# A backbone of mLSTM, RWKV-7, RG-LRU and attention: the recurrence's steps and preparations numbered 300 ahead for every engine but TensorE

## The chip, the cores and the metric

The kernel runs on one core of a Trainium2 chip. The metric is the device time of one execution in microseconds; the kernel before is given by the median of three runs. A profiled execution of the same program gives the trace that is read here.

## The reference, cut to what matters

The kernel computes a two-layer backbone over 512 latent tokens and 256 context tokens of width 1024. Layer 0 projects its input once and feeds two mixers, an mLSTM and an RWKV-7 recurrence; their outputs are concatenated and projected; an MLP of width 4096 follows. Layer 1 has an RG-LRU and a neighbourhood attention in the same arrangement. The part that the change touches is the RWKV recurrence, with 8 heads of 64 in two directions (z), first over the context and then, from the context's state, over the latent tokens:

```python
def rwkv_run(r, v, decay, kk, k_dir, b_vec, S0):
    ...
    def step(S, inp):
        r_t, w_t, k_t, v_t, a_t, b_t = inp
        sa = jnp.einsum('zbhij,zbhj->zbhi', S, a_t)
        S = S * w_t[..., None, :] + sa[..., :, None] * b_t[..., None, :] + v_t[..., :, None] * k_t[..., None, :]
        return S, jnp.einsum('zbhij,zbhj->zbhi', S, r_t)
    S, y = lax.scan(step, S0, xs)
```

Context tokens share every weight with the latent ones: in layer 0 they have their own output projection and their own MLP pass.

## The kernel before, in words

All matrix products of the projections and MLPs are split into a high and a low part (`gemm`, L244): one weight tile of 128 x 1024 is loaded (L235), rounded on ScalarE to `wh` (L237), the rest is formed as `wl` on VectorE or GpSimd (L241), and TensorE then makes three products for each of 8 blocks of 128, that is 24 matmuls into one PSUM bank, of which there are two (`psg`). For the 256 context columns that bank is emptied by VectorE (L338 in output projections and the second half of the MLP, L383 in the first half).

The recurrence is cut into chunks of 64 tokens: 12 chunks, `s` = 0 to 3 for the context and 4 to 11 for the latent tokens, each for both directions. What a chunk needs from its own data alone is made in `pre(s)` (L839): loads from DRAM that `rwkv_in` wrote (L849 to L855), products `psA` (16 matmuls) that ScalarE copies (L861) and VectorE masks (L862, L863), then the inverse of 16 x 16 blocks. For it `AB` goes through DRAM (L868, L869) into `M` (L876), 15 pairs of small dependent operations follow (L890, L892; on GpSimd for `s` up to 4, on VectorE for the 7 chunks after), and the result `Xi` goes through DRAM again (L895) to `Xr` (L897), is transposed (L900) and widened to 64 x 64 by four groups of small matmuls `psI` with VectorE or ScalarE work between them (`dd` L910, `t` L918 and L920, `d1`, and `T` L939). `step(s)` (L949) then carries the state: `psC` products of `AS` and `X`, of `T` and `r`, of `BK` and `X` (the new state `S`, L968, L969), and of `Q` and `ar` for the output `ya_c` or `ya_l` (L985, L988). The tiles of a chunk lie in one of two sets, `s % 2`; those of the inverse exist once (pool `pr`).

Around this lies other work, the fillers (`fillers`, a generator): `rwkv_in(1)` (inputs of the latent chunks), the latent and the context output projection of the mLSTM half (`lat_mlstm`, `ctx_mlstm`), and `ctx_half`, which needs the recurrence's context output: its norms (`rwkv_norms`, L996 to L1004), the gate (`rwkv_gate`, L1024), the other half of the context's output projection, and the context's MLP. The loop over `s` pulls a set amount of filler (`PL`, 21 units from `s` = 3 on, where a context gemm of the MLP counts 2.6), then emits `step(s)`, `rwkv_norms(s)` and `pre(s + 1)`.

This emission order is not the order on the engines. When the program is closed, a scheduler walks a simulated timeline and gives each engine, among its instructions whose inputs are there, the one with the lowest number. The numbers count up in the order of emission. What comes out is one fixed queue for each engine and for the DMA issues of SyncE (SP), and the chip works each queue off in order.

The two lines of the loop that the change wraps are these:

```python
        S = step(s, X, S, Xn)
        rwkv_norms(s)
        ...
            pre(s + 1, Xn)
        X = Xn
        if s >= 3:
            pull(fill, PL[4])
```

Of the kernel before, what the change touches and what calls it, by code (L numbers as in the profile page):

```python
# [3 lines left out]

# [1 line left out]

# [12 lines left out]
P = 128  # L19
# [98 lines left out]
def hybrid_kernel(ctx: ExitStack, tc: tile.TileContext, A, out):  # L118
    WS = [int(x) for x in "2422"]
    nc = tc.nc  # L120
    uid = [0]

    def nm(s):
        uid[0] += 1
        return f"{s}_{uid[0]}"

    def after(ins, first):
        tc.add_manual_dep(ins.ins, first.ins.name,
                          mybir.DependencyInfo(mybir.DependencyClass.NoSync, mybir.DependencyReason.DATA),
                          reason="first matmul of the bank")  # L130

    def mm(o, l, r, start=True, stop=True, shared=False, tile=None):
        kw = {"tile_position": (32 * tile[0], 32 * tile[1])} if tile else {}
        return nc.tensor.matmul(o, l, r, start=start, stop=stop, skip_group_check=shared, **kw)  # L134

    pd = ctx.enter_context(tc.tile_pool(name="pd", bufs=1, space=bass.MemoryType.DRAM))
    pd2 = ctx.enter_context(tc.tile_pool(name="pd2", bufs=2, space=bass.MemoryType.DRAM))
# [9 lines left out]
    ident = C["ident"]  # L147
# [10 lines left out]
    def ada(layer, parts, pa, psa, tag):  # L158
        for pair, half in parts:
            ps = psa.tile([P, 256], F32, tag=tag, name=nm("psada"))  # L160
            for k0 in range(0, NK, 4):

                w = pa.tile([P, 4, D], F32, tag="adaw", name=nm("adaw"))
                for i in range(0, 4, 2):
                    nc.sync.dma_start(w[:, i:i + 2, :], A["ada_w"][layer, pair, half, (k0 + i) // 2])
                for i in range(4):
                    k = k0 + i
                    for j in range(4):
                        mm(ps[32 * j:32 * j + 32, :], sc[:, k, :], w[:, i, 256 * j:256 * j + 256], k == 0, k == NK - 1)
                yield 1.8  # L170
            rows = pa.tile([P, 256], F32, tag="rows", name=nm("rows"), bufs=1)
            nc.vector.tensor_copy(rows, ps)
            pt = psa.tile([P, 2, P], F32, tag=tag, name=nm("pst"))
            for t in range(2):
                nc.tensor.transpose(pt[:, t, :], rows[:, P * t:P * t + P], ident)
            src = pt.rearrange("p t (i j r) -> p i t j r", i=2, j=2)
            for i, idx in enumerate(PAIRS[pair]):
                o = 8 * idx + 4 * half
                dst = mod[:, layer, o:o + 4, :].rearrange("p (j t) c -> p t j c", t=2)
                bo = COLS["ada_b"][0] + 48 * layer + o  # L180
                bias = cols[:, bo:bo + 4].rearrange("p (j t) -> p t j", t=2)
                one = 1.0 if idx in (1, 4) else 0.0
                for cnd in range(2):
                    nc.vector.scalar_tensor_tensor(dst[:, :, :, cnd], src[:, i, :, :, cnd], one, bias, op0=ALU.add, op1=ALU.add)
# [228 lines left out]
    for i in (1, 0):  # L413
        n = SEGS[i][1]
# [87 lines left out]
    with tc.tile_pool(name="pg1", bufs=1) as pg1:  # L502
# [20 lines left out]
        for z in range(2):  # L523
# [37 lines left out]
            for c0, n in ((0, 4), (4, 2)):  # L561
                pt = psm.tile([P, n, P], F32, tag="m", name=nm("pst"))
# [126 lines left out]
    def rwkv_in(si, psp, psh, tag, last=None):  # L689
        off, n, _ = SEGS[si]  # L690
# [3 lines left out]
        fl = lambda a: a.rearrange("p c t -> p (c t)")  # L694
        with tc.tile_pool(name=nm("pha"), bufs=1) as pha, tc.tile_pool(name=nm("ph"), bufs=1) as ph, \
# [32 lines left out]
            for p in range(4):  # L728
                gup = ph.tile([P, P], F32, tag="gup", name=nm("gup"))
                nc.sync.dma_start(gup, A["g_up"][:, P * p:P * p + P])  # L730
                kk, k, r = (ph2.tile([P, nch, 64], F32, tag=a, name=nm(a)) for a in ("kk", "k", "r"))
                v = ph.tile([P, nch, 64], F32, tag="v", name=nm("v"))
# [31 lines left out]
                for z in range(2):  # L764
# [6 lines left out]
                    for kind in range(2):  # L771
# [4 lines left out]
                        o = 8 * z + 4 * kind + p  # L776
                        nc.scalar.activation(t_, pw, AF.Tanh, scale=0.5, bias=DV["upb"][:, o:o + 1])
                        th.append(t_)
                for z in range(2):
# [12 lines left out]
                    bk = ph.tile([P, nch, P], F32, tag="bk", name=nm("bk"))  # L792
# [11 lines left out]
                    nc.sync.dma_start(bkD[si][:, st, z, p, :], bk)  # L804
                pv = psh.tile([P, nb, P], F32, tag=tag, name=nm("psv"))
                for c in range(nb):
                    nc.tensor.transpose(pv[:, c, :], fl(v)[:, P * c:P * c + P], ident)
                vt = pha.tile([P, nb, P], F32, tag="zs", bufs=2, name=nm("vt"))
                nc.scalar.copy(vt, pv)
                nc.sync.dma_start(vD[si][:, p, :].rearrange("(c t) i -> t c i", t=P), vt)  # L810
# [24 lines left out]
    def bank(use, shape):  # L835
        pool, tag, bufs = banks[use]
        return pool.tile(shape, F32, tag=tag, bufs=bufs, name=nm("ps" + use))

    def pre(s, X):  # L839
# [5 lines left out]
        bk = pr2.tile([P, 2, 4, P], F32, tag="bk", name=nm("bk"))  # L845
# [7 lines left out]
        for z in range(2):  # L853
            c = 64 * (ch[z] - s0)
# [26 lines left out]
        for z in range(2):  # L881
            pt = bank("A", [P, 4, P])
            for p in range(4):
                nc.tensor.transpose(pt[:, p, :], bk[:, z, p, :], ident)
            nc.scalar.copy(BK[:, z], pt)
        eng = nc.gpsimd if s <= CT // CR else nc.vector
        for j in range(15):
            n, m = 15 - j, j + 1
# [37 lines left out]
        for p in range(4):  # L926
            for z, q in ((0, 0), (1, 0), (0, 1), (1, 1)):
                g, o = 2 * q + z, 2 * q + 1 - z
# [4 lines left out]
        for p in range(4):  # L933
            for z, q in ((0, 0), (1, 0), (0, 1), (1, 1)):
                o, g = 2 * q + z, 2 * q + 1 - z
# [10 lines left out]
    def new_x(s):  # L946
        return sets[s % 2].tile([P, 2, 4, 2, 64], F32, tag="X", name=nm("X"))

    def step(s, X, S0, Xn):  # L949
        ar, ge, Q, AS, BK, tt = PRE.pop(s)  # L950
        chunk = chunk_of(s)
        pR = bank("C", [P, 2, 4, 64])
        for z, p, q in UNITS:
            mm(pR[hs_[q], z, p, :], AS[:, z, p, q, :], X[:, z, p, q, :])
        r_ = pr.tile([P, 2, 4, 64], F32, tag="r", name=nm("r"))
        nc.scalar.copy(r_, pR)
        pU = bank("C", [P, 2, 4, 64])
        for z, p, q in UNITS:
            mm(pU[hs_[q], z, p, :], tt[z][hs_[q], p, :], r_[hs_[q], z, p, :])
        nc.scalar.copy(X[0:64, :, :, 0, :], pU[0:64])  # L960
        nc.vector.tensor_copy(X[0:64, :, :, 1, :], pU[64:P])
        S1 = None
        if s < NCR - 1:
            pS = bank("C", [P, 2, 4, 64])
            for z, p, q in UNITS:
                mm(pS[hs_[q], z, p, :], BK[:, z, p, hs_[q]], X[:, z, p, q, :])
            S1 = sets[(s + 1) % 2].tile([P, 2, 4, 64], F32, tag="S", name=nm("S"))
            nc.vector.tensor_tensor(S1, pS, S0, op=ALU.add)  # L968
            nc.vector.tensor_tensor(S1, S1, ge[:, :, :, None].to_broadcast([P, 2, 4, 64]), op=ALU.mult)  # L969
            nc.scalar.copy(Xn[0:64, :, :, 0, :], S1[0:64])  # L970
            nc.vector.tensor_copy(Xn[0:64, :, :, 1, :], S1[64:P])
        pY = bank("C", [P, 2, 4, 64])
        first = [None, None]
        for z, p, q in UNITS:
            i1 = mm(pY[hs_[q], z, p, :], Q[:, z, p, q, :], X[:, z, p, q, :], first[q] is None, False, shared=True)
            if first[q] is None:
                first[q] = i1
            else:
                after(i1, first[q])
        for z, p, q in UNITS:  # L980
            mm(pY[hs_[q], z, p, :], ar[hs_[q], z, p, 64:P], S0[hs_[q], z, p, :], False, False, shared=True)
        for z in range(2):
            d = ya_of(chunk[z])
            if chunk[z] in seen:
                nc.vector.tensor_tensor(d, pY[:, z], d, op=ALU.add)  # L985
            else:
                seen.add(chunk[z])
                nc.scalar.copy(d, pY[:, z])  # L988
        return S1
# [16 lines left out]
    def rwkv_norms(s):  # L1006

        si, last = (0, 3) if s < 4 else (1, 11)
        if s in (2, 3, 9, 11):
            v = YA[si].rearrange("p (g c) a i -> p g (c a) i", g=4)  # L1010
            for g in (slice(0, 4, 3) if s == last else slice(1, 3),) if si == 0 else (0, 3) if s == last else (1, 2):
                rwkv_norm(v[:, g] if si == 0 else v[:, g:g + 1])
# [64 lines left out]
    def pull(gen, us):  # L1077

        pos[1] += us
        while pos[0] < pos[1]:  # L1080
            t = next(gen, None)
            if t is None:
                pos[0] = pos[1]
                return
            pos[0] += t

    work = {str(h): mlstm_head(h) for h in range(HM)}
    work["c"] = rwkv_in(0, psg2, psm, "m")
    for o in "0000a0c1ccc1cc11c1c22cc2c23c12ccc33cR33":
        if o == "a":  # L1090
            bg[:] = [itertools.chain(ada(0, ((1, 0), (1, 1), (2, 0), (2, 1)), pa1, psa1, "ada"),
                                     ada(1, ((0, 0), (0, 1), (1, 0), (1, 1)), pa1, psa1, "ada")), 0.5, 0.0]
        elif o == "R":
# [7 lines left out]
            banks.update(A=(psh2, "h", 1), I=(psa1, "ada", 1))  # L1101
            S = sets[0].tile([P, 2, 4, 64], F32, tag="S", name="S0")
            nc.vector.memset(S, 0.0)
            X = new_x(0)
# [28 lines left out]
    for s in range(NCR):  # L1133
        if s < 4:
            pull(fill, PL[1 + s])
        while s == 3 and "in" not in done:
            pos[0] += next(fill)
        Xn = new_x(s + 1) if s + 1 < NCR else None
        while s == 4 and "lat" not in done:
            pos[0] += next(fill) or 0.0  # L1140
        S = step(s, X, S, Xn)
        rwkv_norms(s)
        if s == 3:
            done.add("ctx")
        if Xn is not None:
            pre(s + 1, Xn)
        X = Xn
        if s >= 3:
            pull(fill, PL[4])
# [353 lines left out]
```

## Time and profile before

| | |
|---|---|
| median of 3 runs | 2049.87 us (2041.36, 2049.87, 2053.16) |
| profiled execution | 2049.73 us, span of its trace 2047.9 us |
| TensorE matmul busy | 1925.2 us, 94% of the span |
| VectorE, ScalarE, GpSimd busy | 1052.2, 874.9, 870.1 us (51%, 43%, 42%) |
| mean granted TensorE clock | 0.965 of full |

The span runs from the first to the last instruction. Steps 0 to 11 of the recurrence lie between 432 and 945 us of it. Lines named L134 are the helper through which nearly all matmuls go, so the tiles tell which product it is. Matmuls are pipelined and their ends are modelled.

### The profile page before, as it was taken

The numbers are of one execution on the slowest core, as the hardware profiler recorded it, in microseconds if no ns is written. First come the engines' busy times: TensorE is split into PE (matmuls) and PEld (weight loads), VectorE is DVE, ScalarE is ACT, GpSimd is POOL, SyncE is SP. The second block draws the span as 40 slices with busy tenths as digits, with TensorE's granted clock in tenths as the row PEclk, the third lists the DMA queues.
The fourth block names the chain that finished last, engine by engine and source line by source line (L and its number), as shares of the span: only waits on it lengthen the run. The fifth ranks groups of instructions, "written<-read, shape, count | busy, mean of one in ns | idle before, by whom it ended". The sixth has DMA issues, their size and how long they took to land. (4 is left out here: it accounts for less than half of the span.)

```text
span 2047.9 us, 36663 instructions
## 1 busy us (share of the span) xinstructions
PE 1925.2 (94%) x14860; PEld 1593.9 (78%) x14860; DVE 1052.2 (51%) x1944; ACT 874.9 (43%) x1441; POOL 870.1 (42%) x708
## 2 busy tenths in 40 slices
PE   6899999899887999999999999999999899999998
PEld 5788786767577888888787888888766688888887
DVE  6773645676676766776541221243666664122122
ACT  4443445355544544444442332334655654233232
POOL 1455554435534222233244444435454454444444
PEclk9999998899888999999999999999989899999999
DMA  7356557454585555544443333325211222333232
GB/s 304 106 197 219 177 198 264 122 159 128 142 239 157 144 166 148 149 134 135 160 144 124 102 94 95 101 91 169 67 54 38 62 67 83 103 94 102 93 102 74
DMA packets 173864, 271.60 MB, mean 133 GB/s; under 512 B 77120, under 2 KB 115648, under 8 KB 168576
## 3 DMA queue, kind: packets, MB, share of 16 engines
q1 hardware_dynamic: 166608, 263.76, 41.4%
q10 hardware_dynamic: 7088, 5.51, 0.8%
q8 instruction: 117, 1.92, 0.4%
q14 instruction: 51, 0.42, 0.1%
HBM read 244.06 MB, written 25.17 MB: 131 GB/s over the span
## 5 line engine op out<-in xcount | busy, mean ns | idle before, releaser
L241 POOL TENSOR_TENSOR wl<-w,wh 128x1024 fp32r<-128x1024 f32 (+3 forms) x245 | 555.9, 2272 | 820.6 <-PE psg L134 435.7
L237 ACT CAST wh<-w 128x1024 fp32r<-128x1024 f32 (+3 forms) x319 | 313.2, 985 | 524.8 <-PE psg L134 460.1
L134 PE MATMUL psg<-xh,wh 128*128 128x512 f32 (+1 forms) x1440 | 500.3, 363 | 13.5 <-DVE k L710 3.0
L134 PE MATMUL psg<-xl,wh 128*128 128x512 f32 (+1 forms) x1440 | 498.5, 358 | 1.1 <-DVE xl L335 1.0
L134 PE MATMUL psg<-xh,wl 128*128 128x512 f32 (+1 forms) x1440 | 324.2, 356 | 0.0
L134 PEld LDWEIGHTS psg<-xh,wh 128*128 128x128 f32 x1440 | 273.5, 191 | 64.8 <-issue 13.3
L134 PEld LDWEIGHTS psg<-xl,wh 128*128 128x128 f32 x1440 | 275.7, 191 | 43.9 <-issue 4.9
L134 PEld LDWEIGHTS psg<-xh,wl 128*128 128x128 f32 x1440 | 243.5, 191 | 39.3 <-issue 3.5
L134 PE MATMUL psg<-hh,wh 128*128 128x512 f32 (+1 forms) x800 | 266.2, 350 | 6.4 <-DVE r L383 3.5
L134 PE MATMUL psg<-hl,wh 128*128 128x512 f32 (+1 forms) x800 | 268.1, 349 | 0.9 <-DVE hl L281 0.8
L338 DVE SCALAR_TENSOR_TENSOR res_l<-psg,mod,res_l 128x512 f32<-128x512 f32 (+1 forms) x108 | 74.3, 690 | 274.1 <-PE psg L134 274.0
L134 PEld LDWEIGHTS psg<-hh,wh 128*128 128x128 f32 x800 | 151.4, 190 | 27.8 <-issue 4.1
L134 PEld LDWEIGHTS psg<-hl,wh 128*128 128x128 f32 x800 | 151.7, 190 | 20.6 <-DVE hl L281 1.2
L134 PE MATMUL psg<-hh,wl 128*128 128x512 f32 (+1 forms) x800 | 166.0, 349 | 0.0
L134 PEld LDWEIGHTS psg<-hh,wl 128*128 128x128 f32 x800 | 132.4, 190 | 19.2
L383 DVE TENSOR_SCALAR r<-psg 128x512 f32<-128x512 f32 (+1 forms) x96 | 57.5, 600 | 171.4 <-PE psg L134 171.3
L281 DVE TENSOR_TENSOR hl<-r,hh 128x512 fp32r<-128x512 f32 (+1 forms) x96 | 86.8, 907 | 80.4 <-ACT hh L280 80.4
L384 ACT ACTIVATE r<-r 128x512 f32<-128x512 f32 (+1 forms) x96 | 53.6, 560 | 125.8 <-DVE r L383 125.8
L241 DVE TENSOR_TENSOR wl<-w,wh 128x1024 fp32r<-128x1024 f32 (+1 forms) x74 | 89.4, 1209 | 33.6 <-ACT wh L237 14.1
L134 PE MATMUL psada<-adaw,sc 128*32 128x256 f32 (+1 forms) x896 | 63.0, 386 | 8.4 <-DMA adaw<-in_ada_w_dram 4.8
L134 PE MATMUL psA<-ar,bk 64*128 64x128 f32 x384 | 51.0, 294 | 7.4 <-issue 4.2
L280 ACT CAST hh<-r 128x512 fp32r<-128x512 f32 (+1 forms) x96 | 52.6, 550 | 2.8
(423 smaller groups left out, 2857.6 us busy)
## 6 DMA issues: line engine op xcount, KB each, us to landing
w<-in_w_dram SPq DMA_DIRECT2D x192, 512.0 KB, 3.7
adaw<-in_ada_w_dram SPq DMA_DIRECT2D x40, 1024.0 KB, 7.4
w<-in_ev_in_dram SPq DMA_DIRECT2D x47, 512.0 KB, 3.7
w<-in_od_in_dram SPq DMA_DIRECT2D x32, 512.0 KB, 3.6
adaw<-in_ada_dram SPq DMA_DIRECT2D x16, 512.0 KB, 11.3
w<-in_out_w_dram SPq DMA_DIRECT2D x32, 256.0 KB, 2.9
bk<-bkD SPq DMA_DIRECT2D x12, 512.0 KB, 6.4
ar<-arD SPq DMA_DIRECT2D x12, 512.0 KB, 4.6
```

The costliest lines, as they stand in the source:

```text
L134: return nc.tensor.matmul(o, l, r, start=start, stop=stop, skip_group_check=shared, **kw)
L237: nc.scalar.copy(wh, w)
L241: eng.tensor_tensor(wl, w, wh.bitcast(F32), op=ALU.subtract)
L280: nc.scalar.copy(h, x)
L281: nc.vector.tensor_tensor(l, x, h.bitcast(F32), op=ALU.subtract)
L338: nc.vector.scalar_tensor_tensor(r_, ps, modcol(layer, idx, m, cnd), r_, op0=ALU.mult, op1=ALU.add)
L383: nc.vector.tensor_scalar(r_, ps, 0.0, None, op0=ALU.max)
L384: nc.scalar.activation(r_, r_, AF.Square)
```

## The change

`ahead(n)` opens a block in which the counter that numbers instructions is set back by `n`; at its end the counter is put back to where it stood before the block. `step` and `pre` are emitted in such blocks with `n` = 300. Inside them each matmul (and the two kinds of transposes on TensorE that `rwkv_in` and `pre` make) is emitted in a block of its own with the opposite offset, so that it gets the counter without the 300. No instruction is added, removed or changed in shape. Two things follow from the counter being put back. A matmul that goes through `mm`, anywhere in the kernel, no longer moves the counter on. And what is emitted after `step` or `pre` starts from the number at which that block began.

```diff
+    lead = [0]
+
+    @contextmanager
+    def ahead(n):
+
+        lead[0] = n
+        with tc.high_priority(offset=n):
+            yield
+        lead[0] = 0
+
     def mm(o, l, r, start=True, stop=True, shared=False, tile=None):
         kw = {"tile_position": (32 * tile[0], 32 * tile[1])} if tile else {}
-        return nc.tensor.matmul(o, l, r, start=start, stop=stop, skip_group_check=shared, **kw)
+        with tc.high_priority(offset=-lead[0]):
+            return nc.tensor.matmul(o, l, r, start=start, stop=stop, skip_group_check=shared, **kw)
...
                 for c in range(nb):
-                    nc.tensor.transpose(pv[:, c, :], fl(v)[:, P * c:P * c + P], ident)
+                    with tc.high_priority(offset=-lead[0]):
+                        nc.tensor.transpose(pv[:, c, :], fl(v)[:, P * c:P * c + P], ident)
...
             for p in range(4):
-                nc.tensor.transpose(pt[:, p, :], bk[:, z, p, :], ident)
+                with tc.high_priority(offset=-lead[0]):
+                    nc.tensor.transpose(pt[:, p, :], bk[:, z, p, :], ident)
...
-        S = step(s, X, S, Xn)
+        with ahead(300):
+            S = step(s, X, S, Xn)
         rwkv_norms(s)
         if s == 3:
             done.add("ctx")
         if Xn is not None:
-            pre(s + 1, Xn)
+            with ahead(300):
+                pre(s + 1, Xn)
```

## Rows read from the trace of the kernel before

**Rows 1.** The page's first part: busy time of each engine over the span.
```profile
span 2047.9 us, 36663 instructions
...
PE 1925.2 (94%) x14860; PEld 1593.9 (78%) x14860; DVE 1052.2 (51%) x1944; ACT 874.9 (43%) x1441; POOL 870.1 (42%) x708
```

**Rows 2.** Busy time by stretch: length, engines, granted clock, DMA share, GB/s.
```profile
400.00:675.00 275.00, 238.28 (x2822) 190.18 (x2823) 186.98 (x344) 130.06 (x234) 121.62 (x213) 0.91 0.56 160
675.00:945.00 270.00, 258.32 (x3930) 240.60 (x3929) 182.54 (x442) 120.31 (x205) 68.98 (x38) 0.99 0.53 148
```

**Rows 3.** TensorE's waits from 400 to 675 us: total us, times, longest.
```profile
PE psg L134 <- DVE gb L1024: 4.9, 1, 4.9
PE psg L134 <- ACT xhom L280: 4.6, 1, 4.6
PE psI L134 <- DMA Xr<-invD: 4.6, 3, 2.9
...
PE psA L134 <- DVE ms L997: 2.4, 1, 2.4
PE psI L134 <- DVE t L920: 2.3, 1, 2.3
```

**Rows 4.** TensorE's waits from 675 to 945 us.
```profile
PE psg L134 <- DVE r L383: 3.5, 3, 1.7
PE psI L134 <- DMA Xr<-invD: 2.9, 3, 1.7
PE psC L134 <- DVE X L961: 1.8, 1, 1.8
PE psC L134 <- DVE T L939: 1.4, 1, 1.4
```

**Rows 5.** Timeline of TensorE around chunk 3: start us, us, instruction.
```profile
560.83 0.65 PE L134 MATMUL psI<-Xt,AB 32*32 32x32 f32 x32
...
568.48 0.45 PE L134 MATMUL psI<-Xt,dd 32*32 32x32 f32 x32
568.75 0.48 PE L134 MATMUL psI<-Xr,dd 32*32 32x32 f32 x32
...
588.82 1.15 PE L134 MATMUL psC<-r,T 64*64 64x64 f32 x32
...
593.75 1.15 PE L134 MATMUL psC<-X,BK 128*64 128x64 f32 x32
```

**Rows 6.** Timeline of VectorE around chunk 3.
```profile
562.84 0.41 DVE L910 TENSOR_TENSOR dd<-psI,cst 128x256 f32<-128x256 f32 x1
...
573.83 0.28 DVE L918 TENSOR_TENSOR t<-psI,Xt 128x128 f32<-128x128 f32 x1
...
584.45 0.60 DVE L939 SCALAR_TENSOR_TENSOR T<-psI,cst,T 128x128 f32<-128x128 f32 x2
...
599.11 0.69 DVE L968 TENSOR_TENSOR S<-psC,S 128x512 f32<-128x512 f32 x1
```

**Rows 7.** Timeline of VectorE over one inverse of a latent chunk.
```profile
817.97 2.25 DVE L890 TENSOR_TENSOR tm<-M,Xi 64x15 f32<-64x15 f32 x1 [3.34 <-DMA M<-dA]
...
824.04 0.22 DVE L892 TENSOR_TENSOR Xi<-Xi,tm 64x63 f32<-64x63 f32 x1
824.30 0.22 DVE L890 TENSOR_TENSOR tm<-M,Xi 64x64 f32<-64x64 f32 x1
...
830.97 2.19 DVE L892 TENSOR_TENSOR Xi<-Xi,tm 64x28 f32<-64x28 f32 x1
...
833.40 0.17 DVE L892 TENSOR_TENSOR Xi<-Xi,tm 64x15 f32<-64x15 f32 x1
```

**Rows 8.** Timeline of GpSimd at the same place.
```profile
830.72 2.40 POOL L241 TENSOR_TENSOR wl<-w,wh 128x1024 fp32r<-128x1024 f32 x1 [10.54 <-ACT wh L237]
```

**Rows 9.** Timeline of TensorE inside a context gemm.
```profile
817.40 0.28 PE L134 MATMUL psg<-hh,wh 128*128 128x256 f32 x1
817.52 0.28 PE L134 MATMUL psg<-hl,wh 128*128 128x256 f32 x1
```

**Rows 10.** TensorE's groups by shape from 945 to 980 us: busy us, mean ns, idle before.
```profile
L134 PE MATMUL psg<-hl,wh 128*128 128x256 f32 x60 | 15.5, 293 | 0.1
```

More of the change, by code (lines that the diff above doesn't have):

```diff
@@ L2 @@
 import math
-from contextlib import ExitStack
+from contextlib import ExitStack, contextmanager
 import numpy as np
```

## The prediction

> **What bounds the kernel now.** I read the page's first part, then the busy times by stretch, then who TensorE waits for, then the timelines of TensorE and VectorE around one chunk of the recurrence. The first shows TensorE with a matmul under way for 94% of the span and every other engine at about half [rows 1]. So the end is set by TensorE's work and by the stretches in which it has none, and since the change adds and removes no instruction, only those stretches and TensorE's clock can move.
>
> By stretch, the 545 us in which the recurrence runs fall in two [rows 2]. From 400 to 675 us (chunks 0 to 3, with the latent inputs and the two first output projections as filler) TensorE is idle 275 - 238.3 = 36.7 us, and its mean granted clock is 0.91: (1 - 0.91) x 275 = 24.8 us of full-clock time are lost between the levels of 2.4 and 1.2 GHz. From 675 to 945 us (chunks 4 to 11, with the context's MLP as filler) it is idle 270 - 258.3 = 11.7 us at a clock of 0.99. In this second stretch TensorE itself is nearly full: a chunk takes 270 / 8 = 34 us, and the recurrence being quicker would only exchange filler for filler.
>
> The Trainium skill ("Trainium Kernel Development and Optimization", Performance Expectations) calls matmul busy time a bad measure of the room left and the busy time of weight loads a good one. By that the second stretch has 270 - 240.6 = 29.4 us of room and not 11.7 [rows 2]; the waits below add up to the 11.7, so the sum goes by them.
>
> Who TensorE waits for tells which idle time the change can reach. Waits that end on something that `step` or `pre` made, or on a bank that they hold: 4.6 for `Xr`, 2.4 for a bank behind the norm's `ms`, 2.3 for `t` [rows 3], 2.9 for `Xr`, 1.8 for `X`, 1.4 for `T` [rows 4], together 15.4 us. The others are the fillers' own: 4.9 for the gate's `gb`, 4.6 for the projection's first `xhom` [rows 3], 3.5 for the MLP's `r` [rows 4] and smaller ones.
>
> **The change, part by part.** *The 300 on VectorE, ScalarE, GpSimd and the DMA issues.* A filler gemm emits 4 to 7 instructions that are not matmuls, and only these now move the counter, so 300 is more than 40 gemms: wherever an instruction of `step` or `pre` is ready, it goes before any filler. What that takes out is time in the queues. Around chunk 3: `psI` ends at 560.83 + 0.65 = 561.48 and `dd` starts 1.4 us later; the next `psI` ends at 569.23 and `t` starts 4.6 us later; `psC` with `BK` ends at 594.90 and `S` starts 4.2 us later. That is 10.2 us behind fillers on VectorE. On TensorE, `psI` starts 5.2 us after `dd` is done (563.25), and the product with `T` 3.8 us after `T` (585.05): 9.0 us that the change leaves [rows 5, 6]. So 10.2 / 19.2 = 53% of the delay in such a chain goes away.
>
> The inverse on VectorE gains too: it takes 817.97 to 833.57, 15.6 us, and its 30 operations follow each other at 0.26 us where nothing comes between, 7.8 us [rows 7]. Of the difference some 4 us are two operations of 2.2 us instead of 0.2, one of them beside a `wl` of 2.40 us on GpSimd that began just before it [rows 7, 8]. I allow one such hold, so 9.8 us and 5.8 us gained per chunk; the longest wait for `Xr`, which hangs on this, is 2.9 us [rows 3].
>
> The Trainium skill ("SBUF — State Buffer", Who interferes with whom) says that a VectorE instruction with two SBUF inputs and a GpSimd instruction that reads SBUF exclude each other for the whole instruction. By that both holds stay, the inverse shrinks to 11.8 and not 9.8 us, and with the lower end of the first term below the sum would be 9 us and not 12; the long operation beside GpSimd's `wl` agrees with it [rows 7, 8].
>
> First term: of the 15.4 us of waits, 53% (8.2) if the rest of the chain waits as before, all of it if being earlier is enough everywhere. I take 11, a little under the middle, because half of the 15.4 are landings of `Xr` of at most 2.9 us each, shorter than the 5.8 us that the inverse gains, but in the first stretch most inverses are on GpSimd, where I have no such gain.
>
> Second term: the gate's 4.9 us. An earlier end of chunk 3 lets norms and gate start earlier, but the norms are not wrapped and go behind `step(4)` and `pre(4)`. Bounds 0 and 4.9; I take 1. For `xhom` and the other fillers' waits I take 0: they can go either way by an operation or two.
>
> Third term: the clock. The first stretch has 9.3 of the 15.4, so 11 x 9.3 / 15.4 = 6.6, with the gate 7.6 of the 36.7 us idle; the same share of 24.8 us is 5.1. Bounds 0 and 5.1; I take 3, since the second stretch shows 11.7 us of idle time at almost no loss of clock [rows 2].
>
> Fourth term, a cost: filler's `psg` banks wait for VectorE. With all 30 operations ahead of them, L338 and L383 can stand behind a run of 7.8 + 2 = 9.8 us. Meanwhile TensorE can fill two banks, each 24 matmuls 0.12 us apart [rows 9], 2 x 2.9 = 5.8 us, and run the four products of a step at 1.15 us each [rows 5], 4.6 us. With these the run is covered; without them 4.0 us are bare, and 7 such inverses cost 28 us. Bounds 0 and 28; I take 3, as the step does stand in that place (its `S` work lies amid the inverse's operations).
>
> *ScalarE, GpSimd and SP.* The copies `AB`, `BK`, `r`, `X` go ahead of the weights' rounding, the inverses of chunks 1 to 4 ahead of GpSimd's `wl`, and the 17 DMA issues of a `pre` ahead of weight loads. I cost these at nothing: the cover is three weight tiles in flight and engines that are 47% and 44% busy in the stretches where they are busiest [rows 2]. If it were gone, the wait would be for `wh` or `wl`, and neither is among TensorE's waits now. In SP's queue a DMA that waits for `Xi` would hold the weights behind it, as it can now.
>
> *TensorE's own order.* It is not left alone. `pre` counts 65 instructions of its own before its first `psI`, and its matmuls are numbered from where the block began, as is the filler pulled after it (8 gemms, 32 to 56 numbers). Before, all of `pre` stood ahead of that filler; now its `psI` stand behind it. I cost it at nothing as long as the recurrence does not end too late: what is left of the context's MLP at 945 us covers it, 60 matmuls with `hl` at 8 to a gemm, 7.5 gemms [rows 10] of 2.9 us, about 22 us.
>
> Sum, against the profiled execution of 2049.73 us: 11 + 1 + 3 - 3 = 12 us less, 2037.7 us. That execution lies 0.1 us from the median of the runs (2049.87), so no correction.
>
> **The rivals.** *Nothing that can be measured.* TensorE's order in the second stretch is full, and in the first the fillers' chains (gate, `xhom`, context norms) take the place of each wait removed. For it: of the 18.8 us of its larger waits 9.5 are the fillers' (4.9 and 4.6), and the change sends these behind [rows 3]. Against it: the 10.2 us of chunk 3 [rows 5, 6]. Time: the terms cancel to within 5 us, 2045 to 2052.
>
> *Slower: banks held behind the inverse.* The fourth term at its upper bound, 28 us, takes the place of 3: 2049.7 - 15 + 28 = 2063 us. It decides from 15 / 7 = 2.1 us bare per inverse on. For it: the MLP's wait for `r` is already the largest in the second stretch, 3.5 us in 3 waits [rows 4]. Against it: the step's products in the same place.
>
> *Slower: the preparation falls behind on TensorE.* Each of the four groups of `psI` lets one gemm of 2.9 us pass: 11.6 us a chunk, half of it on the path since two chunks are in flight, times 8 latent chunks, 46 us. Beyond the cover of 22 us, 24 us are bare, less the 12: 2062 us. It decides when the last step ends later than about 967 us. For it: the numbering. Against it: `psI` runs amid filler already, and TensorE's 9.0 us of chunk 3 [rows 5, 6] came about with the better numbers.
>
> **How the numbers follow.** Forecast 0.48, nothing 0.22, banks 0.18, TensorE's order 0.12. A measurement of this kernel can tell about 0.5%, 10 us, from no change. Of the forecast, own range 2024 (all terms at their best, 15.4 + 4.9 + 5.1 = 25.4) to 2046, 0.38 lie over 10 us faster and 0.10 within; of the banks 0.16 lie slower and 0.02 within, of TensorE's order 0.11 and 0.01. So faster 0.38, same 0.35, slower 0.27. The range goes from 2020 (best terms, and a little for runs that spread by 12 us) to 2066 (the two slower rivals).
>
> **What would show it.** Right: in the trace after, `dd`, `t` and `S` start within 1 us of the product they need, an inverse on VectorE takes about 10 us, the waits for `Xr`, `t`, `X` and `T` are under 5 us together, the last step ends before 945 us, and 400 to 675 us hold less idle time at a clock above 0.91. Wrong: waits of `psg` for L338 or L383 that grow by more than 2 us per latent chunk; a last step after 967 us; waits for `wh` or `wl` that were not there; or idle time outside 400 to 1060 us that moves, which would mean that the new counting of matmuls has changed the order where nothing was wrapped.

## The result, and the profile after

The change is slower: 2083.19 us (median of 4 runs, 2081.74 to 2087.69) against 2046.41 us (4 runs, 2041.36 to 2053.16), a ratio of 1.0172 with a 95% interval of 1.0149 to 1.0194. The forecast was 2038 us, faster than before, and its range ended at 2066; the measured time lies beyond that end. The profiled execution of after took 2082.05 us.

The page's first part, to be held against [rows 1]:

```profile
span 2080.2 us, 36659 instructions
...
PE 1950.4 (94%) x14860; PEld 1609.9 (77%) x14860; DVE 1057.0 (51%) x1944; ACT 872.4 (42%) x1441; POOL 867.6 (42%) x708
```

The span grew by 32.3 us. Of these TensorE is idle for only 7.1 (129.8 against 122.7) and busy for 25.2 more, with the same 14860 matmuls. The prediction looked for the gain in idle time and let the busy time move by the clock alone. By stretch, against [rows 2], and then one slice of 25 us:

```profile
400.00:675.00 275.00, 237.94 (x2781) 189.62 (x2783) 182.22 (x339) 129.56 (x233) 122.32 (x220) 0.90 0.55 157
675.00:945.00 270.00, 257.43 (x3322) 232.88 (x3313) 167.66 (x388) 103.08 (x178) 63.56 (x35) 0.91 0.50 137
775.00:800.00 25.00, 24.95 (x109) 18.16 (x109) 5.58 (x11) 4.37 (x8) 2.35 (x1) 0.50 0.19 49
```

In the first stretch busy time and clock are as before, with 41 matmuls less. In the second TensorE is as busy as before and gets 608 matmuls less done (3322 against 3930), at a clock of 0.91 and not 0.99. From 775 to 800 us it is busy for 24.95 of 25 us, at the lower of its two levels throughout, and does 109 matmuls. Over the whole span the mean granted clock falls from 0.965 to 0.959. By that, as an estimate, (1 - 0.965) x 2047.9 = 71.7 us of full-clock time are lost before and (1 - 0.959) x 2080.2 = 85.3 after, so some 14 of the 32 us stand beside a lower clock. What TensorE does from 775 to 800 us, in its timeline:

```profile
780.71 0.31 PE L145 MATMUL psI<-Xr,AB 32*32 32x32 f32 x2
780.96 0.58 PE L145 MATMUL psg<-xl,wh 128*128 128x256 f32 x1
781.47 0.31 PE L145 MATMUL psI<-Xr,AB 32*32 32x32 f32 x2
781.71 0.58 PE L145 MATMUL psg<-xh,wh 128*128 128x256 f32 x1
...
801.06 0.53 PE L145 MATMUL psI<-Xt,AB 32*32 32x32 f32 x18
```

Two matmuls of the inverse, one of the MLP, two of the inverse, one of the MLP, 0.75 us a turn. The 64 matmuls of that bank, 32 of which took 0.65 us in one piece in [rows 5], last from 780.71 to 801.59, with the 16 `psA` of the next chunk among them. So VectorE's `dd` starts 36 us after `Xt`, where the kernel before has 2.1 us at the same chunk. After, then before:

```profile
766.66 0.45 DVE L913 STREAM_TRANSPOSE Xt<-Xr 128x256 f32<-128x256 f32 x1 [3.27 <-DMA Xr<-invD]
...
802.64 0.42 DVE L923 TENSOR_TENSOR dd<-psI,cst 128x256 f32<-128x256 f32 x1
```

```profile
758.59 0.45 DVE L900 STREAM_TRANSPOSE Xt<-Xr 128x256 f32<-128x256 f32 x1 [3.50 <-DMA Xr<-invD]
...
760.72 0.42 DVE L910 TENSOR_TENSOR dd<-psI,cst 128x256 f32<-128x256 f32 x1
```

TensorE's waits, against [rows 3] from 400 to 675 us, and then against [rows 4] from 675 to 945 us:

```profile
PE psI L145 <- DMA Xr<-invD: 6.8, 2, 3.4
PE psg L145 <- ACT xhmc L291: 5.0, 1, 5.0
PE psst L145 <- DVE acc L319: 4.9, 1, 4.9
...
PE psg L145 <- DVE gb L1037: 0.9, 1, 0.9
```

```profile
PE psA L145 <- DMA ar<-arD: 5.5, 3, 2.8
...
PE psg L145 <- DVE res_c L349: 0.6, 1, 0.6
PE psg L145 <- DVE r L394: 0.5, 1, 0.5
```

The sum hardly moved, and new names stand in it; `ar`, the load for the next chunk's scores, was not there before. The last product of the recurrence begins at 987.66 us, 45 us later than before. After, then before:

```profile
987.66 1.15 PE L145 MATMUL psC<-S,ar 64*64 64x64 f32 x32
```

```profile
942.48 1.15 PE L134 MATMUL psC<-S,ar 64*64 64x64 f32 x32
```

### The profile page after: what moved, and what is told of

Read it like the earlier page. It is cut to its first block, busy times and chain, and to the rows that moved or that the text cites. A ratio compares the mean times of both kernels' runs of the same rounds, so it can differ in the third digit from the quotient of the medians.

```text
span 2080.2 us, 36659 instructions
## 1 busy us (share of the span) xinstructions
PE 1950.4 (94%) x14860; PEld 1609.9 (77%) x14860; DVE 1057.0 (51%) x1944; ACT 872.4 (42%) x1441; POOL 867.6 (42%) x708
## 5 line engine op out<-in xcount | busy, mean ns | idle before, releaser
L145 PE MATMUL psg<-xh,wl 128*128 128x512 f32 (+1 forms) x1440 | 329.7, 359 | 0.0
L349 DVE SCALAR_TENSOR_TENSOR res_l<-psg,mod,res_l 128x512 f32<-128x512 f32 (+1 forms) x108 | 74.2, 689 | 273.6 <-PE psg L145 273.6
L394 DVE TENSOR_SCALAR r<-psg 128x512 f32<-128x512 f32 (+1 forms) x96 | 57.5, 601 | 196.1 <-PE psg L145 196.0
L145 PE MATMUL psA<-ar,bk 64*128 64x128 f32 x384 | 62.4, 317 | 12.3 <-DMA ar<-arD 5.5
L145 PEld LDWEIGHTS psA<-ar,bk 64*128 64x128 f32 x384 | 51.1, 213 | 19.8 <-issue 6.8
```

The source lines that it names most:

```text
L349: nc.vector.scalar_tensor_tensor(r_, ps, modcol(layer, idx, m, cnd), r_, op0=ALU.mult, op1=ALU.add)
L394: nc.vector.tensor_scalar(r_, ps, 0.0, None, op0=ALU.max)
```

## The experiments

The theory after this: the lead of 300 is not the loss; TensorE's new numbering is. Rivals: the lead itself, matmuls without numbers, and a preparation that is merely late. Ratios are to the kernel before on the same chip; its median there was 2046 to 2052 us, so a ratio says more than a difference of medians. The last two columns are of the profiled runs: TensorE's busy time, and how often, from 400 to 1120 us, a matmul's form on the array (the rows and columns that it uses, in the trace 128\*128, 64\*128, 32\*32 and others) differs from that of the one before, counted in one execution of each.

| run | median us | ratio (95%) | busy us | changes of form |
|---|---|---|---|---|
| before | 2046.41 | 1 | 1925.2 | 331 |
| after | 2083.19 | 1.0172 (1.0149 to 1.0194) | 1950.4 | 408 |
| e1_pe_as_before | 2040.91 | 0.9958 (0.9936 to 0.9980) | 1919.8 | 328 |
| e1b_pe_as_before_1500 | 2050.45 | 1.0013 (0.9998 to 1.0029) | 1922.5 | 334 |
| e2_offset0 | 2085.95 | 1.0162 (1.0113 to 1.0211) | 1958.0 | 398 |
| e3_uncounted | 2051.28 | 0.9999 (0.9978 to 1.0020) | 1928.0 | 329 |
| e6_moved_on | 2055.43 | 1.0024 (1.0009 to 1.0038) | 1924.6 | 333 |
| e9_put_back | 2149.80 | 1.0468 (1.0448 to 1.0489) | 2038.8 | 631 |
| e10_put_back_together | 2057.82 | 1.0031 (1.0014 to 1.0047) | 1929.4 | 314 |
| e5_together | 2061.95 | 1.0068 (1.0044 to 1.0092) | 1928.4 | 310 |
| e12_late | 2067.88 | 1.0090 (1.0055 to 1.0126) | 1926.9 | 308 |
| e14_together_on_time | 2066.97 | 1.0080 (1.0068 to 1.0093) | 1935.6 | 319 |
| e15_together_early | 2067.35 | 1.0083 (1.0068 to 1.0099) | 1934.2 | 328 |
| e11_before_together | 2052.77 | 1.0008 (0.9989 to 1.0026) | 1915.5 | 290 |
| e4_all_ahead | 2106.38 | 1.0254 (1.0221 to 1.0287) | 1944.5 | 302 |
| e13_best | 2073.14 | 1.0101 (1.0076 to 1.0126) | 1919.4 | 287 |

### Which of its parts is the loss

**The lead without TensorE's part** (e1_pe_as_before, e1b_pe_as_before_1500). TensorE keeps the numbers of the kernel before, the other engines are 300 ahead, then 1500.

```diff
-        with tc.high_priority(offset=n):
-            yield
+        tc.cur_priority -= n
+        yield
+        tc.cur_priority += n
...
-        with tc.high_priority(offset=-lead[0]):
+        with put_back():
```

`put_back` here adds the lead to the counter for one matmul and takes it off again.

> TensorE's instructions keep the numbers of the kernel before, all other engines' instructions of step and pre are numbered 300 ahead. Theory (the loss is TensorE's order: preparation matmuls numbered among the filler's, alternating one by one with them): the loss of 37 us is gone, 2035 to 2056 us, psI's 32 matmuls in one piece of 0.5 us. Rival 1 (banks held behind VectorE's inverse): 2070 to 2090 us, waits of psg for L338/L383's successors over 10 us. Rival 2 (the recurrence late on TensorE): also 2035 to 2056 us.

> The same with 1500 in place of 300: where matmuls count, 300 is about 10 filler gemms and 1500 over 50, as in the changed kernel. Theory: as the one with 300, within 15 us of it, 2030 to 2060 us. Rival 1: slower than the one with 300, 2070 to 2095 us, for then every filler eviction stands behind the inverse. Rival 2: 2030 to 2060 us.

With 300: 0.42% faster, TensorE idle 111.6 us of its span of 2031.4 (122.7 before). Its second stretch:

```profile
675.00:945.00 270.00, 260.28 (x3889) 241.95 (x3889) 189.71 (x447) 119.04 (x204) 70.31 (x38) 1.00 0.54 152
```

With 1500 nothing is left (1.0013). Here matmuls count, and by the expectation above 300 reaches over some 10 gemms and 1500 over more than 50, as the 300 of the change does. So a lead of the change's reach brings nothing that can be measured, and the shorter one a little. The lead is not the loss; how much lead pays was not settled.

**The change without the lead** (e2_offset0).

```diff
-        with ahead(300):
+        with ahead(0):
```

> The changed kernel with 0 in place of 300: the counter is put back after step and pre and matmuls are not counted, but nothing is numbered ahead. Theory (TensorE's order): nearly the whole loss is there, 2068 to 2095 us, with stretches in which psI and psg alternate at a clock of 0.5. Rival 1 (banks held behind VectorE): no loss, 2040 to 2055 us. Rival 2 (recurrence late): 2065 to 2095 us.

The whole loss is there (1.0162), so it comes from the numbering that the blocks bring, and not from the 300.

**Only the matmuls without numbers, nothing ahead, counter never put back** (e3_uncounted).

```diff
-        with ahead(300):
-            S = step(s, X, S, Xn)
+        S = step(s, X, S, Xn)
...
-            with ahead(300):
-                pre(s + 1, Xn)
+            pre(s + 1, Xn)
```

> Nothing runs ahead and the counter moves on as before; only the matmuls of the recurrence and the other matmuls of that helper take no number of their own. If leaving the matmuls unnumbered spoils TensorE's order, this has the loss of 1.6 to 1.7% (about 2082 us, clock of 675:945 near 0.91). If the loss needs the counter put back, TensorE switches between banks of the inverse and others as often as before (98 times) and the time is within 0.3% of before (2043 to 2055 us), with the last step's state at about 940 us.

Nothing (0.9999).

**The change with the counter moved on behind each block** (e6_moved_on).

```diff
         lead[0] = n
-        with tc.high_priority(offset=n):
-            yield
+        tc.cur_priority -= n
+        yield
+        tc.cur_priority += n
         lead[0] = 0
```

> The change as it is, but behind each step and preparation the counter is moved on by what they issued on the other engines instead of being put back. If the putting back is the loss, this gives the whole loss back and keeps the gain seen with TensorE numbered as before: 2038 to 2050 us, clock of 675:945 near 0.99, no single matmuls of the inverse between single ones of the MLP. If the unnumbered matmuls are the loss, it stays near 2080 us.

1.5 of the 1.72 points (per cent of the time before) are gone, but the time lies above the 2050 us expected, for the gain of 0.42% is not kept. With a lead of the same reach and numbered matmuls it was 1.0013. So the lead itself is worth little, of either sign; that the sign hangs on how TensorE's order falls was not tried.

**Only the putting back, in the kernel before** (e9_put_back).

```diff
+        p0 = tc.cur_priority
+        yield
+        tc.cur_priority = p0
...
+        with put_back():
             S = step(s, X, S, Xn)
...
+            with put_back():
                 pre(s + 1, Xn)
```

> The kernel before, every instruction numbered, nothing ahead, but the counter is put back to where it stood after each step and each preparation, so that the MLP pulled next gets the same numbers as the preparation. If the putting back alone is the loss, this is slower by at least what the change lost (2080 us or more): on TensorE's queue the banks of the scores and of the state change places with others 318 and 356 times instead of 118 and 150, more than in the change, so that by the price of single matmuls between others it may be 2100 us or more, with a clock below 0.95 in 675:945. If only together with the unnumbered matmuls, it is within 0.5% of before.

4.68% slower, with no lead and every matmul numbered. So the putting back is the loss. Its timeline shows the price of a turn before the clock falls:

```profile
704.80 0.33 PE L141 MATMUL psC<-X,AS 128*64 128x64 f32 x2
705.06 0.39 PE L141 MATMUL psg<-xl,wh 128*128 128x256 f32 x1
705.37 0.33 PE L141 MATMUL psC<-X,AS 128*64 128x64 f32 x2
705.63 0.38 PE L141 MATMUL psg<-xh,wh 128*128 128x256 f32 x1
```

A turn of `psg` and two `psC` takes 705.63 - 705.06 = 0.57 us. In one piece the `psg` takes 0.12 [rows 9] and a pair of `psC` some 0.06 (16 pairs in 1.15 us, [rows 5], of which the last matmul's own time is 0.22). The other 0.39 us stand at two changes of form, some 0.20 each. The same kernel has a control, transposes of the form 128\*128 in turn with `psg` of that form:

```profile
774.64 0.27 PE L891 MATMUL psA<-cst,bk 128*128 128x128 f32 x1
774.66 0.36 PE L141 MATMUL psg<-hh,wh 128*128 128x256 f32 x1
774.87 0.27 PE L891 MATMUL psA<-cst,bk 128*128 128x128 f32 x1
774.89 0.37 PE L141 MATMUL psg<-hl,wh 128*128 128x256 f32 x1
```

0.23 us a turn, and in one piece 0.12 and 0.11 (four such transposes take 0.60 us in the run below, the last one 0.27): taking turns costs nothing, changing the form does. Nor is it the type of the operands: in the kernel those of `psg` are F32R and those of `psC` F32, and those of the transposes are F32 too. That a change of form costs time is what the Trainium skill says ("TensorEngine Tiling (Array Packing)", Tiling Modes, Key Properties): a change of tiling mode, not of the tile alone, drains TensorE. The trace agrees and puts some 0.2 us on it.

### How the putting back loses the time

**The same, with each bank's matmuls together** (e10_put_back_together). Once the first matmul of a bank of the recurrence or its preparation is issued, the others follow at once (`behind`: numbered 2000 lower; `group`: tied behind the first). The edit at one bank, the others likewise:

```diff
-                    mm(pj[b32[g], z, p, :], dd[b32[g], z, p, :], tt[z][b32[g], p, :], tile=(g, g))
+                    with behind(g0):
+                        g0 = group(mm(pj[b32[g], z, p, :], dd[b32[g], z, p, :], tt[z][b32[g], p, :], tile=(g, g)), g0)
```

> The putting back alone (all numbered, nothing ahead), which is 4.7% slower, with one thing added: once the first matmul of a psum bank of the recurrence or of its preparation is issued, the rest of the bank follows at once. On TensorE's queue the switches of the scores' and the state's banks go from 318 and 356 to 128 and 100; the first product of the inverse starts behind nearly the same matmuls of the MLP (2021, 2224, 2437 of them against 2028, 2250, 2419). If single matmuls of different tiles in turn are the loss, at least four fifths of it go: 2035 to 2060 us and a clock above 0.95 in 675:945. If the order of the work, that is a late preparation, is the loss, it stays above 2110 us.

1.0468 becomes 1.0031: 4.4 of the 4.7 points come back, some 90 us, for 317 changes of form less. Busy time falls by 109.4 us, 0.35 us a change, the lower clock included. Its share is large: by the mean clocks (0.936 in 2148.5 us, 0.962 in 2057.8 us) some 59 us of full-clock time, an estimate as above. From 675 to 945 us the clock is back, as expected. Only put back, then together:

```profile
675.00:945.00 270.00, 264.48 (x2867) 220.77 (x2867) 136.81 (x332) 87.06 (x153) 46.96 (x29) 0.80 0.40 111
```

```profile
675.00:945.00 270.00, 255.42 (x3785) 238.15 (x3778) 179.28 (x431) 115.53 (x198) 64.75 (x36) 0.97 0.52 144
```

The banks in one piece:

```profile
693.53 1.16 PE L141 MATMUL psA<-ar,bk 64*128 64x128 f32 x8
...
700.65 0.60 PE L908 MATMUL psA<-cst,bk 128*128 128x128 f32 x4
...
710.61 1.15 PE L141 MATMUL psC<-X,AS 128*64 128x64 f32 x32
```

**The change itself, with the preparation's banks together** (e5_together; `psA` and `psI`).

```diff
-                    mm(pa_[:, p, :], bk[hs_[q], z, p, :], ar[hs_[q], z, p, :])
+                    with behind(g0):
+                        g0 = group(mm(pa_[:, p, :], bk[hs_[q], z, p, :], ar[hs_[q], z, p, :]), g0)
```

> The changed kernel, but once the first matmul of a psA or psI group is issued the others of the group follow it on TensorE at once; where a group begins is numbered as in the changed kernel. Theory (alternation of single matmuls is what costs): most of the loss is gone, 2040 to 2062 us, clock from 675 to 945 us back to 0.97 or more. Rival 2 (it is the lateness of the preparation that costs): 2070 to 2090 us. Rival 1 (VectorE): 2070 to 2090 us.

1.0172 becomes 1.0068, and busy time falls by 22.0 us for 98 changes less, 0.22 each; the clock from 675 to 945 us goes from 0.91 to 0.97. So about 1.0 of the 1.7 points go with the matmuls in turn, their lower clock included. TensorE's and VectorE's timelines at chunk 7 show what is left:

```profile
776.09 3.09 PE L145 MATMUL psA<-ar,bk 64*128 64x128 f32 x16 [4.86 <-DMA ar<-arD]
...
781.75 0.65 PE L145 MATMUL psI<-Xr,AB 32*32 32x32 f32 x32
```

```profile
765.22 0.45 DVE L926 STREAM_TRANSPOSE Xt<-Xr 128x256 f32<-128x256 f32 x1 [3.67 <-DMA Xr<-invD]
...
782.81 0.42 DVE L938 TENSOR_TENSOR dd<-psI,cst 128x256 f32<-128x256 f32 x1 [0.73 <-PE psI L145]
```

The bank is one piece again, but starts 16 us after `Xt` is done. Chunk 8's scores have come in front of chunk 7's inverse in the queue, and TensorE stood 4.86 us for their `ar` with the inverse's data there.

**Lateness alone, in the kernel before** (e12_late): the inverse's first product is numbered 800 later, its bank in one piece.

```diff
-                    mm(pi[b32[g], z, p, :], AB[b32[g], z, p, b32[g % 2]], ti[z][b32[g], p, :], tile=(g, g))
+                    with later(-2000 if g0 else 800):
+                        g0 = group(mm(pi[b32[g], z, p, :], AB[b32[g], z, p, b32[g % 2]], ti[z][b32[g], p, :], tile=(g, g)), g0)
```

> The kernel before, but the inverse's first product of each preparation is numbered 800 later, its 32 matmuls together: on TensorE's queue it starts behind 60 to 170 more matmuls of the MLP (7 to 20 us), in the last chunks later than in the change (2600, 2764, 2984, 3176 of them against 2576, 2707, 2960, 3091), and nothing is in turn. If lateness of the preparation is the loss, 2065 to 2090 us. If the matmuls in turn are, within 0.5% of before (2040 to 2060 us), although the last step's state comes 15 us or more later.

1.0090: I had expected either nothing or the whole loss, and it is half. The last product of the recurrence begins at 960.17 us, 17.7 later than before, and busy time is as before (1926.9): the loss is idle time, 135.0 us against 122.7.

**Putting the start back in the change** (e14_together_on_time, e15_together_early), banks together and their first matmul 20 lower, then 80.

```diff
-        with tc.high_priority(offset=2000 if first else 0):
+        with tc.high_priority(offset=2000 if first else 20):
```

> The change with each bank of the preparation together (which left 0.68%), and the first matmul of each such bank numbered 20 lower, so that on TensorE's queue the inverse's first products start where they did in the kernel before (2024, 2264, 2456, 2648, 2840 matmuls of the MLP ahead of them against 2028, 2241, 2424, 2629, 2837; without the 20 it is 2144, 2313, 2576, 2707, 2960). If the 0.68% is lateness, it goes: 2040 to 2056 us, the last step's state by 945 us, no wait for ar in the second stretch. If it is something else that the change did, it stays at 2058 to 2068 us.

> The same with 80 instead of 20: the inverse's first products start 30 to 120 matmuls of the MLP (4 to 14 us) earlier than in the kernel before. If only lateness costs, this is no slower than with 20, and the recurrence ends before 930 us. If TensorE's order must fit the moment at which the data come, being early costs too, as with everything 300 ahead on TensorE (2.5% slower): above 2065 us, with TensorE idle more than 45 us in 400 to 675 us.

1.0080 and 1.0083: no gain from either. With 20 the place in the queue is that of the kernel before, but TensorE gets there late: `psC<-X,BK` of chunk 4 begins at 678.91 us against 661.06, the recurrence's last product at 966.03 and not by 945, and 4.1 us of waits for `ar` are still there. With 80 the time is the one expected if being early costs, but not the sign named for it: idle time from 400 to 675 us is 33.9 us and not over 45. From 675 to 1000 us TensorE waits 10.7 us for `Xr`, 2.9 before. So the 0.68% can't be put down to the start of the inverse alone. Which part of the order makes it stays open.

**The kernel before with banks together** (e11_before_together), those of the step and the transposes too.

```diff
-            mm(pR[hs_[q], z, p, :], AS[:, z, p, q, :], X[:, z, p, q, :])
+            with behind(g0):
+                g0 = group(mm(pR[hs_[q], z, p, :], AS[:, z, p, q, :], X[:, z, p, q, :]), g0)
```

> The kernel before with the same rule, each bank's matmuls together. It has some single matmuls in turn too (118 and 150 switches, here 102 and 102). By the price of a switch from the loss of the change (some 35 us for 94 switches more to and from the inverse and the scores, so 0.2 to 0.4 us each) this gives back 10 to 25 us at most: 2025 to 2045 us. If what is in turn in the kernel before costs nothing, it is within 0.3%.

1.0008, where I expected 10 to 25 us. The changes saved are real (41 less, busy time 9.7 us less), but idle time grows by more: 139.4 us against 122.7 in a span that is 7.0 us longer. TensorE's waits for `Xr` from 400 to 945 us go from 7.5 to 12.4 us. That a bank held together keeps the MLP out while its data come is argued from this, not tried.

### Two versions that should have been better

**Everything 300 ahead, TensorE too** (e4_all_ahead).

```diff
-        lead[0] = n
+        lead[0] = 0
```

> The change with TensorE included: step and preparation 300 ahead on every engine, the counter put back, matmuls without numbers of their own. If the loss is that the preparation's matmuls slip one by one between the MLP's because both have the same numbers, being 300 ahead parts them: each goes as soon as its data are there, 106 switches of the inverse's banks against 162, 2035 to 2055 us, and the last step's state earlier than before (before 935 us). If the lead on the other engines or the uncounted matmuls are the loss it stays at 2070 to 2090 us.

1.0254, slower than the change and than both ranges named, with fewer changes of form than before (302). Here much of the loss is waiting: TensorE is idle for 158.6 us, 122.7 before. TensorE's largest wait from 400 to 675 us:

```profile
PE psg L145 <- ACT xhmc L291: 17.4, 1, 17.4
```

TensorE is busy for 224.0 of those 275 us (238.3 before), at a clock of 0.84.

**The lead of the first run, with banks together** (e13_best), its edits put on the kernel before with banks together.

```diff
-        S = step(s, X, S, Xn)
+        with ahead(300):
+            S = step(s, X, S, Xn)
```

> TensorE numbered as before, the other engines 300 ahead, which gained 0.4%, and each bank's matmuls together. If both gains add, it is 2 to 15 us faster than with the lead alone: 2025 to 2040 us, the fastest of these. If the lead gained by the same matmuls in turn (142 and 116 switches against 150 and 118), it is no faster than the kernel before with banks together.

1.0101. Busy time is that of the first run (1919.4), and TensorE idle 152 us, among it one wait of 14.2 for `xhmc`. The two edits don't add; why that wait opens was not followed up. The lead without TensorE's part stays the fastest version.

## Why the prediction was wrong

The step that failed is "TensorE's own order", costed at nothing "as long as the recurrence does not end too late". It is the loss: without the lead 1.0162, with the counter moved on 1.0024, with nothing but the putting back 1.0468. The passage named the cause rightly (the counter put back, `psI` numbered among or behind the filler pulled after) and asked only how late the recurrence would end, with 22 us of MLP as cover. It missed that matmuls with neighbouring numbers are dealt out one by one, and that this costs TensorE's own time, some 0.2 us at each change of form and a clock of 0.91 and not 0.99 from 675 to 945 us: the cover doesn't help against MLP matmuls that themselves take longer. About 1.0 of the 1.7 points are of this kind; the other 0.7 came with the new order too, and which part of it makes them stays open.

- *First term, 11 us less.* Half right. In chunk 3 `dd`, `t` and `S` follow their products by 1.9, 0.9 and 0.0 us, 2.8 together where [rows 5, 6] had 10.2:

```profile
571.17 0.45 PE L145 MATMUL psI<-Xt,AB 32*32 32x32 f32 x32
...
577.60 0.45 PE L145 MATMUL psI<-Xr,dd 32*32 32x32 f32 x30
...
596.84 0.47 PE L145 MATMUL psC<-X,BK 128*64 128x64 f32 x2 [0.42 <-ACT X L973]
...
603.48 0.22 PE L145 MATMUL psC<-X,BK 128*64 128x64 f32 x1
```

```profile
573.48 0.41 DVE L923 TENSOR_TENSOR dd<-psI,cst 128x256 f32<-128x256 f32 x1
...
578.90 0.28 DVE L931 TENSOR_TENSOR t<-psI,Xt 128x128 f32<-128x128 f32 x1
...
603.74 0.69 DVE L981 TENSOR_TENSOR S<-psC,S 128x512 f32<-128x512 f32 x1 [2.98 <-PE psC L145]
```

  But at the last of the three the gain is none: the product of `X` and `BK`, 1.15 us in one piece in [rows 5], now runs from 596.84 to 603.70 with other matmuls in between. So `S` starts 6.9 us after its product's start, and 5.4 before. What VectorE gave there, TensorE's order took.

  And the inverse did not shrink: the six whole ones after 690 us take 15.3 us on average before and after, not 9.8. One of them, with GpSimd beside it, against [rows 7, 8]:

```profile
803.31 0.17 DVE L903 TENSOR_TENSOR tm<-M,Xi 64x15 f32<-64x15 f32 x1
...
806.54 0.42 DVE L394 TENSOR_SCALAR r<-psg 128x256 f32<-128x256 f32 x1 [2.42 <-PE psg L145]
806.88 2.19 DVE L903 TENSOR_TENSOR tm<-M,Xi 64x39 f32<-64x39 f32 x1
...
815.75 2.40 DVE L905 TENSOR_TENSOR Xi<-Xi,tm 64x48 f32<-64x48 f32 x1
...
819.95 0.17 DVE L905 TENSOR_TENSOR Xi<-Xi,tm 64x15 f32<-64x15 f32 x1
```

```profile
806.64 2.38 POOL L252 TENSOR_TENSOR wl<-w,wh 128x1024 fp32r<-128x1024 f32 x1 [23.58 <-PE psg L145]
814.77 3.32 POOL L252 TENSOR_TENSOR wl<-w,wh 128x1024 fp32r<-128x1024 f32 x1 [5.76 <-ACT wh L248]
```

  Fillers still stand between its operations, one of them waiting 2.42 us for TensorE. A number chooses among what is ready, and an operation that hangs on the one just ahead of it isn't ready when the engine comes free (argued from the queue, not tried). Both operations of over 2 us lie beside a `wl` on GpSimd; the prediction had allowed for one. It had read one such hold in the trace before, where the first long operation of [rows 7], at 817.97, lay beside a `wl` as well:

```profile
817.81 2.37 POOL L241 TENSOR_TENSOR wl<-w,wh 128x1024 fp32r<-128x1024 f32 x1 [9.65 <-DMA M<-dA]
```

  The Trainium skill says of this pair, a VectorE instruction with two SBUF inputs and a GpSimd instruction that reads SBUF, that they contend ("SBUF — State Buffer", Who interferes with whom). The traces agree.
- *Second and third term, gate and clock.* The gate's wait fell by 4.0 us, and `xhmc` (5.0) and `acc` (4.9, 1.7 before) took its place, as the rival "nothing" had it. That the clock of the second stretch could fall, as it did from 0.99 to 0.91, was no term of the sum. The first stretch's clock is 0.90, not above 0.91.
- *Fourth term, banks held behind the inverse.* Not there: the waits for L349 and L394 from 675 to 945 us are 0.6 and 0.5 us; the one for `r` alone was 3.5 [rows 4].
- *The rival "the preparation falls behind on TensorE"* had the right place, and its sign came (last step past 967 us). Its price, 2062 us, was one of lateness alone, and all that isn't matmuls in turn is 0.68 of 1.72 points. Its chance of 0.12 was too low for the one step in which the numbering changed for the worse.
- What the lead was thought to bring, 12 us, is nothing with a lead of the change's reach when TensorE's numbers are left alone (1.0013). With the shorter reach it is 0.42% or 8.6 us; that this is near the 12 us is luck, for the inverses take 15.3 us there too.

## What to carry to other kernels

When a change moves priorities, read first what it does to the fixed order on the engine that bounds the kernel: matmuls of different forms with interleaved numbers were a cost here, even though TensorE showed as fully busy. Count in the trace how often the form changes, and matmuls per stretch beside busy time. Keeping banks in one piece is a repair where they were torn (some 90 and 21 us here), and it was no gain by itself in the kernel before.

## What had not been expected of the hardware

A change of form costs about 0.2 us at the full clock, and turns at the same form nothing, by the turns shown above. TensorE is shown busy all through, and its granted clock falls nevertheless. These are three stretches of 8 us of the kernel that only puts back: the first with 168 matmuls, the others, mostly in turn, with 63 and 54.

```profile
696.00:704.00 8.00, 7.89 (x168) 6.03 (x168) 4.28 (x10) 3.51 (x7) 0.62 (x1) 1.00 0.51 174
704.00:712.00 8.00, 8.00 (x63) 5.34 (x62) 0.85 (x2) 0.63 (x2) 0.00 (x0) 0.69 0.01 2
712.00:720.00 8.00, 8.00 (x54) 5.72 (x53) 2.35 (x7) 2.36 (x4) 0.00 (x0) 0.50 0.21 49
```

The clock goes from 2.4 to 1.2 GHz in the second, while TensorE shows no idle time. That the turns bring it down is what these rows suggest, and with the banks together the clock came back in both kernels (0.80 to 0.97, 0.91 to 0.97 from 675 to 945 us). But the order of the work changed with them, and with everything 300 ahead the clock was 0.88 there with few changes of form; so the turns alone were not isolated.
